# Queueing the rotary multiply-adds behind the next projection piece, not right after the half copies that feed them

## The chip, the cores and the metric

The kernel runs on the eight cores of one Trainium2 chip; each core computes one sequence of the batch with the same program, and no core talks to another. The metric is the device time of the slowest core, in microseconds (us). Most executions agree within 0.3%, but some fall into a slower state in which one die has a lower granted clock. Engines are called PE (matrix multiply), DVE (vector), ACT (scalar activation), POOL (GpSimd) and SP (sync). The granted clock is the share of PE's full clock that its throttle let through, as the trace records it. The program gives each engine its own queue of instructions, in the order in which it emits them.

## The reference

A decoder layer: normalisation, one combined input projection, two kinds of attention side by side, an output projection, and an MLP. This study touches the part below: eight heads of attention over all earlier positions with a forget bias ("fox"), and eight query heads plus two key heads that are rotated ("rope") for sliding-window attention.

```python
def rope(x, pos):                 # rotate-half over 128 dimensions, half = 64
    ...
    x1, x2 = xf[..., :half], xf[..., half:]
    out = jnp.concatenate([x1 * cos - x2 * sin, x2 * cos + x1 * sin], axis=-1)

def reference(...):
    h = rmsnorm(x, g_pre_mix) * (1.0 + sc_a) + sh_a
    proj = h @ w_in                                  # 2048 x 2048 by 2048 x 4616, per sequence
    fq, fk, fv, fg, sq, sk, sv = split(proj)
    fox = forgetting_attention(fq, fk, fv, log_f)    # 8 heads, causal
    sq = rope(sq); sk = rope(sk)                     # 8 + 2 heads: ten "stripes" of 128 columns
    swa = sliding_window_sink_attention(sq, sk, sv, sinks)
    x = x + gt_a * rmsnorm(concat(fox, swa) @ w_out, g_post_mix)
    ...                                              # squared-ReLU MLP
```

## The kernel before

The program interleaves two streams. The attention of fox heads 0 and 1 is the steady stream; each of its steps has a score matmul (PE), a subtraction of the forget bias (DVE), an exponential (ACT) and two matmuls that use it (PE). Between these, a filler emits pieces of the projections: one piece is four matmuls, and a 512-column tile of a stripe takes four pieces.

```python
    def fox(segs):                           # LA = 3 steps of lookahead
        ...
            if i + LA < n:
                begin(i + LA)                # score matmul into a bank of SF = [2, 3, 5]
            F.fill(w)                        # w = 5.6 matmuls: 1 or 2 pieces
            pv(L[i])                         # two matmuls that use exp of step i
            if i + LA < n:
                expo(L[i + LA])              # DVE subtraction, then ACT exp
            F.fill(w)

    def g_fm(slot, t, evac, rel):            # one tile of a projection stripe, in 4 pieces
        bk = next_pj()                       # projection banks 0 and 1 in turn
        for q in range(4):
            pe([... 4 matmuls into bk ...])
            if q == 3:
                ...
                evac(bk)
            yield 4
```

The rotary evacuation of a tile is the function that was changed. ACT copies the two halves crosswise into `rot`; then DVE makes two multiply-adds (each adds the bias and multiplies by the cosine or the sine) and an addition of them.

```python
    def ev_rope(i, dstf):
        def mk(t):
            ...
            def ev(bk):
                rot, cs = rots[rp[0] % 2], sqb[rp[0] % 2]
                rp[0] += 1
                act(rot(p=(0, 64)), bk(p=(64, 128)), AF.Copy)
                act(rot(p=(64, 128)), bk(p=(0, 64)), AF.Copy)
                stt(cs(), bk(), bs(slice(i, i + 1)), cosT(sl), ALU.add, ALU.mult)
                stt(rot(), rot(), bsw(slice(i, i + 1)), sinT(sl), ALU.add, ALU.mult)
                tt(dstf(sl), cs(), rot(), ALU.add)
            return ev
        return mk
```

At a stripe's start, its bias column is computed by 16 one-column matmuls into the bank that the next score matmul will use, and copied out by DVE (the "bias copy", `bs`). That score matmul must wait for this copy.

```python
    def sw_bias(i, b):
        bk = fm_col(b, banks[SF[St.sb % 3]])          # calls col(): 16 small matmuls
        cp(bs(slice(i, i + 1)), bk(0, 1))             # DVE: the bias copy
        act(bsw(...), bs(...), AF.Copy)               # ACT, twice: the halves crosswise
        ...
```

The order on DVE follows from this: score subtractions, rotary ops and bias copies stand in one queue, and an instruction whose input is late holds up all that follow. What counts as late is set by the program: its `op()` makes a reader of a PSUM bank (where matmul results land) wait for the last reader of that bank on another engine. So the first rotary op waits for both half copies, although it uses nothing that they write.

The softmax here doesn't subtract the row's maximum and nothing guards it: scores larger than these inputs give would overflow.

Of the kernel before, what the change touches and what calls it, by code (L numbers as in the profile page):

```python
# [9 lines left out]
ALU = mybir.AluOpType  # L10
# [328 lines left out]
def program(nc, stack, orders, dry, T):  # L339
# [20 lines left out]
    shb, bq, bqb, bs, bsw, bvb, bsv, wob = (B[n] for n in ("shb", "bq", "bqb", "bs", "bsw", "bvb", "bsv", "wob"))  # L360
# [3 lines left out]
    cosT, sinT = B["cosT"], B["sinT"]  # L364
# [15 lines left out]
    def mm(out, lhsT, rhs, start, stop):  # L380
        return (out.ap, lhsT.ap, rhs.ap, start, stop)

    def pe(mms, r, w, extra=()):
        def fn(e):
            ins = None
            for (o, l, rh, st, sp) in mms:
                ins = e.matmul(o, lhsT=l, rhs=rh, start=st, stop=sp)  # L387
            return ins
        return P.op("pe", fn, r, w, extra=extra)

    def act(out, in_, func, bias=None, scale=1.0):
        r = [in_]
        kw = {}
        if isinstance(bias, Acc):
            r.append(bias)
            kw["bias"] = bias.ap
        elif bias is not None:
            kw["bias"] = bias
        if isinstance(scale, Acc):
            r.append(scale)  # L400
            kw["scale"] = scale.ap
        else:
            kw["scale"] = scale
        return P.op("act", lambda e: e.activation(out=out.ap, in_=in_.ap, func=func, **kw), r, [out])  # L404

    def tt(out, a, b, op, eng="dve"):
        return P.op(eng, lambda e: e.tensor_tensor(out=out.ap, in0=a.ap, in1=b.ap, op=op), [a, b], [out])  # L407

    def stt(out, a, s, b, op0, op1, eng="dve"):
        r = [a, b] + ([s] if isinstance(s, Acc) else [])  # L410
        sc = s.ap if isinstance(s, Acc) else s
        return P.op(eng, lambda e: e.scalar_tensor_tensor(out=out.ap, in0=a.ap, scalar=sc, in1=b.ap, op0=op0, op1=op1),  # L412
                    r, [out])
# [6 lines left out]
    def cp(out, a):  # L420
        return P.op("dve", lambda e: e.tensor_copy(out=out.ap, in_=a.ap), [a], [out])  # L421
# [121 lines left out]
    def next_pj():  # L543
        b = banks[PJ[pj[0] % 2]]
        pj[0] += 1
        return b
# [13 lines left out]
    def g_v(slots, bp, dst, rel, add=None):  # L560
        bk = next_pj()
        for bi in range(2):
            blk = 2 * bp + bi
            t, o = blk // 4, (blk % 4) * 128
            for q in range(2):
                b = R1.bufs[slots[q]]
                pe([mm(bk(bi * 256, bi * 256 + 256), hT(t, 8 * q + kk, slice(o, o + 128)), b(slice(kk * 256, kk * 256 + 256)),
                       q == 0 and kk == 0, q == 1 and kk == 7) for kk in range(8)],
                   [b()] + [hT(t, slice(8 * q, 8 * q + 8))], [bk()])
                if bi == 1 and rel:  # L570
                    R1.rel(slots[q])
                if bi == 1 and q == 1:
                    src = bk()
                    src = src.re(src.ap.rearrange("p (a d) -> p a d", a=2))
                    if add is None:
                        cp(dst(slice(2 * bp, 2 * bp + 2)), src)
                    else:
                        tt(dst(slice(2 * bp, 2 * bp + 2)), src, add().re(add.h[:].unsqueeze(1).broadcast_to([128, 2, 256])), ALU.add)
                yield 4


    def col(out, slot_bufs, lhs):

        bk = out or next_pj()
        pe([mm(bk(0, 1), lhs(k), shb(slice(k, k + 1)), k == 0, k == KC - 1) for k in range(KC)], slot_bufs + [shb()], [bk()])
        return bk

    def fm_col(b, out=None):
        return col(out, [b()], lambda k: b(slice(k * 128, k * 128 + 128)))
# [27 lines left out]
    def ev_rope(i, dstf):  # L617
        def mk(t):
            sl = slice(t * TS, t * TS + TS)

            def ev(bk):
                rot, cs = rots[rp[0] % 2], sqb[rp[0] % 2]
                rp[0] += 1
                act(rot(p=(0, 64)), bk(p=(64, 128)), AF.Copy)
                act(rot(p=(64, 128)), bk(p=(0, 64)), AF.Copy)
                stt(cs(), bk(), bs(slice(i, i + 1)), cosT(sl), ALU.add, ALU.mult)
                stt(rot(), rot(), bsw(slice(i, i + 1)), sinT(sl), ALU.add, ALU.mult)
                tt(dstf(sl), cs(), rot(), ALU.add)
            return ev
        return mk  # L630

# [7 lines left out]
    def v_col(p, s):  # L639
        for hh in range(2):  # L640
            bk = col(None, [R1.bufs[x]() for x in s],
                     lambda k: R1.bufs[s[k // 8]](slice((k % 8) * 256 + hh * 128, (k % 8) * 256 + hh * 128 + 128)))
            cp(bvb(slice(2 * p + hh, 2 * p + hh + 1)), bk(0, 1))
# [13 lines left out]
        yield 2  # L657

    def svpair():
        s = [R1.acq(("A", I_SV)), R1.acq(("A", I_SV + 1))]  # L660
        bk = next_pj()
        pe([mm(bk(0, 256), shb(slice(k, k + 1)).re(shb.h[:, k:k + 1].broadcast_to([128, 128])),
               R1.bufs[s[k // 8]](slice((k % 8) * 256, (k % 8) * 256 + 256)), k == 0, k == KC - 1) for k in range(KC)],
           [R1.bufs[x]() for x in s] + [shb()], [bk()])
        cp(bsv(), bk(0, 256))
        for bp in range(8):
            yield from g_v(s, bp, vts, bp == 7, bsv)
# [10 lines left out]
    class Fill:  # L678
        def __init__(self):
            self.main = []  # L680
            self.side = []
            self.every = 4
            self.n = 0
            self.pend = []
            self.credit = 0.0

        def _one(self):
            while self.main:
                try:
                    v = next(self.main[0])  # L690
                except StopIteration:
                    self.main.pop(0)
                    continue
                self.n += 1
                if self.n % self.every == 0:
                    self._side()
                return v
            return None
# [20 lines left out]
        def drain(self):  # L719
            while self.main:  # L720
                self._one()
            self.credit = 0.0

        def drain_side(self):
# [3 lines left out]
    F = Fill()  # L728
# [384 lines left out]
    def qk_(h):  # L1113
# [3 lines left out]
        for t in range(NT):  # L1117
# [4 lines left out]
    F.every = 6  # L1122
    F.side = [mods(g, F.pend) for g in range(2, 6)]
    fox([(0, lambda: [sk_(0), svpair(), sq_(0), sq_(1), sq_(2), sq_(3)], 64 * 5 + 128, 0),
         (1, lambda: [sk_(1), sq_(4), sq_(5), sq_(6), sq_(7), qk_(2)], 64 * 7, 0)])
    F.drain()
# [241 lines left out]
def build():  # L1368
# [117 lines left out]
    with ExitStack() as stack:  # L1486
        T["banks"] = [Bank(stack.enter_context(nc.psum_tensor(f"bank{i}", [128, 512], F32)), i) for i in range(8)]
        orders = program(nc, stack, {}, True, T)
        program(nc, stack, orders, False, T)
# [49 lines left out]
```

## Time and profile before

| | before |
|---|---|
| time, median of 3 executions | 3128.81 us (3125.04 to 3580.78, the last slow) |
| the stretch: first bias copy to first sliding-window matmul, mean of 8 cores | 320.1 us |
| PE idle in it (core 3) | 34.9 us |
| DVE waiting for half copies in it (core 3) | 105.9 us |

From the page of the kernel before: busy time and its share of the span, then the span in 40 slices (tenths busy; granted PE clock in tenths), then the engines' shares of the chain that ended last.

```profile
PE 2913.8 (93%) x15016; PEld 1375.2 (44%) x15016; DVE 928.1 (30%) x1489; ACT 748.4 (24%) x1224; POOL 469.1 (15%) x614
...
PE   2799989999999899999999999999999999999993
...
PEclk9899989999999899999999999999999999999996
...
PE 82%; DVE 5%; DMA 4%; ACT 4%; issue 3%; POOL 1%; SPq 0%; DVEq 0%; ACTq 0%; POOLq 0%
```

PE has work for 93% of the time. The stretch with the rotary stripes is slices 3 to 7, counted from 0 (a slice is 78 us); in the middle of it, in slice 5, both the PE row and the clock row show an 8.

The windows view of core 3 over the stretch. Columns: busy time and instructions of each engine, granted clock, DMA share, GB/s.

```profile
core 3: us, PE busy (x) PEld busy (x) DVE busy (x) ACT busy (x) POOL busy (x), PEclk, DMA share, GB/s
273.50:595.90 322.40, 287.49 (x1625) 137.41 (x1624) 146.29 (x240) 110.34 (x197) 25.36 (x48) 0.91 0.49 85
```

PE is busy 287.5 of 322.4 us at a mean clock of 0.91; DVE is busy 45% and ACT 34%.

The waits view of the same stretch, PE first (who waited for whom, us in total, times, longest), then DVE.

```profile
PE bank L387 <- DVE bs L421: 23.0, 8, 5.0
PE bank L387 <- DVE sq_207 L412: 6.2, 2, 3.2
PE bank L387 <- DVE modT L407: 3.8, 2, 3.4
```

```profile
DVE sq_206 L412 <- ACT qrot L404: 63.7, 20, 8.0
DVE sq_207 L412 <- ACT acc_208 L404: 42.2, 20, 2.7
```

Two thirds of PE's idle time ends with a copy of 128 single values. DVE waits 105.9 us for half copies, 40 times. (`sq` is the tile that the first rotary op writes, `qrot` and `acc` are the two buffers for `rot`; `modT` holds modulation vectors that the filler computes as a side job.)

The chain of waits of the kernel before shows one rotary tile, from one exponential to the next (start us, length us, what; some tiny hand-overs left out).

```profile
371.69 0.45 ACT Pb_101 L404
...
372.40 0.59 ACT acc_208 L404
...
373.01 0.60 ACT acc_208 L404
...
373.70 0.75 DVE sq_207 L412
374.45 0.67 DVE acc_208 L412
...
375.22 0.10 DVE mix L407
...
375.83 0.70 DVE bank L407
...
376.61 0.55 ACT Pb_102 L404
```

ACT makes an exponential (Pb), then the two half copies (acc is one of the two buffers for `rot`); only then DVE can make its three rotary ops, and only after these the score subtraction (bank) that the next exponential needs. One turn takes 4.92 us (371.69 to 376.61), and each engine is idle for most of the other's part.

The PE timeline at the first stripe boundary (in brackets, the idle time before an instruction and what ended it).

```profile
356.43 0.54 PE L387 MATMUL bank<-shb,ring_69 128*128 128x1 bf16 x16
356.83 1.02 PE L387 MATMUL bank<-hT,ring_69 128*128 128x512 bf16 x4
361.37 0.58 PE L387 MATMUL bank<-qT_72,kT_73 128*128 128x512 bf16 x1 [3.51 <-DVE bs L421]
361.75 1.91 PE L387 MATMUL bank<-hT,ring_69 128*128 128x512 bf16 x4
```

The bias column ends at 356.8 us, a projection piece follows, then PE stands still for 3.51 us until the bias copy is done, and afterwards four matmuls take 1.91 us instead of 1.02.

### The profile page before, as it was taken

What the parts mean: (1) busy time and instruction counts of PE and PEld (TensorE: products, weight loads), DVE (VectorE), ACT (ScalarE), POOL (GpSimd) and SP (SyncE); (2) the same over time, 40 slices, a digit from 0 to 9 for tenths busy, and PEclk for the clock granted to TensorE, in tenths of its full rate; (3) what the DMA queues carried; (4) which work ended last, traced back from release to release, by engine and by line L of the source; (5) the groups of instructions that cost most, each with busy time, mean ns of one, the idle gap of its engine ahead of it and who ended that gap; (6) DMA issues with size and microseconds to landing.
All of it is one profiled execution on the core that took longest, in us unless ns stands there. A gap on an engine that the chain in (4) does not pass through costs nothing.

```text
span 3124.7 us, 38905 instructions; the slowest of 8 cores (3109.0 to 3124.7 us)
## 1 busy us (share of the span) xinstructions
PE 2913.8 (93%) x15016; PEld 1375.2 (44%) x15016; DVE 928.1 (30%) x1489; ACT 748.4 (24%) x1224; POOL 469.1 (15%) x614
## 2 busy tenths in 40 slices
PE   2799989999999899999999999999999999999993
PEld 1336533466444344444444444444444444444441
DVE  1323445345555456642111000000233211000005
ACT  1312333454555435532111000000111111000000
POOL 1010000000001155520000011111100000111114
PEclk9899989999999899999999999999999999999996
DMA  9855545433646324354444455555788544444455
GB/s 185 215 90 104 101 75 88 78 61 59 112 85 102 77 95 157 127 130 74 78 78 74 82 100 95 96 92 96 162 189 191 92 75 78 77 75 77 78 99 197
DMA packets 99782, 327.92 MB, mean 105 GB/s; under 512 B 12144, under 2 KB 12272, under 8 KB 93200
## 3 DMA queue, kind: packets, MB, share of 16 engines
q0 software_dynamic: 58896, 213.97, 41.6%
q1 hardware_dynamic: 40704, 111.46, 10.2%
q8 instruction: 122, 2.00, 0.3%
q14 instruction: 60, 0.49, 0.1%
HBM read 497.32 MB, written 42.01 MB: 173 GB/s over the span
## 4 chain that ended last, share of the span: by engine, by line
PE 82%; DVE 5%; DMA 4%; ACT 4%; issue 3%; POOL 1%; SPq 0%; DVEq 0%; ACTq 0%; POOLq 0%
PE bank L387 82%; DVE bank L407 1%; POOL acc_209 L407 1%; DMA xstA<-xP 1%; DMA xstB<-xP 1%; DMA rmod_87<-wMA 1%; ACT acc_208 L404 1%; DVE mixF L412 1%; ACT rr L404 1%; DMA cfb_82<-crow 1%; ACT qrot L404 1%; DMA rsh_90<-wMB 0%; DVE bank L412 0%; DVE sq_207 L412 0%; DVE acc_208 L412 0%
## 5 line engine op out<-in xcount | busy, mean ns | idle before, releaser
L418 DVE TENSOR_SCALAR bank<-bank 128x512 f32<-128x512 f32 x256 | 166.1, 695 | 638.4 <-PE bank L387 638.4
L421 DVE COPY mixF<-bank 128x512 f32<-128x512 f32 x64 | 41.3, 686 | 842.8 <-PE bank L387 842.8
L387 PE MATMUL bank<-mix,rung_130 128*128 128x512 bf16 x1024 | 226.2, 379 | 0.0
L387 PE MATMUL bank<-mix,rung_127 128*128 128x512 bf16 x1024 | 226.2, 379 | 0.0
L387 PE MATMUL bank<-mix,rung_128 128*128 128x512 bf16 x1024 | 226.2, 379 | 0.0
L387 PE MATMUL bank<-mix,rung_129 128*128 128x512 bf16 x1024 | 226.2, 379 | 0.0
L404 ACT ACTIVATE sq_206<-bank 128x512 f32<-128x512 f32 x30 | 17.9, 598 | 792.9 <-DVE mixF L421 792.9
L387 PEld LDWEIGHTS bank<-mix,rung_129 128*128 128x128 bf16 x1024 | 100.2, 98 | 121.5 <-issue 1.1
L387 PEld LDWEIGHTS bank<-mix,rung_127 128*128 128x128 bf16 x1024 | 100.3, 98 | 120.7
L387 PEld LDWEIGHTS bank<-mix,rung_128 128*128 128x128 bf16 x1024 | 100.4, 98 | 120.7
L387 PEld LDWEIGHTS bank<-mix,rung_130 128*128 128x128 bf16 x1024 | 99.9, 98 | 121.5 <-issue 0.6
L407 DVE TENSOR_TENSOR bank<-bank,cfb_82 128x512 f32<-128x512 f32 x192 | 117.3, 629 | 85.2 <-PE bank L387 80.6
L387 PE MATMUL bank<-hT,ring_69 128*128 128x512 bf16 x512 | 139.6, 404 | 3.2 <-DVE sq_207 L412 3.2
L387 PE MATMUL bank<-hT,ring_71 128*128 128x512 bf16 x384 | 101.7, 394 | 0.4 <-DVE kT_73 L421 0.4
L407 POOL TENSOR_TENSOR acc_208<-acc_208,sq_206 128x512 f32<-128x512 f32 x62 | 78.6, 1267 | 113.1 <-ACT sq_206 L404 113.0
L407 DVE TENSOR_TENSOR bank<-bank,cfb_80 128x512 f32<-128x512 f32 (+3 forms) x128 | 73.5, 594 | 39.2 <-PE bank L387 39.2
L407 POOL TENSOR_TENSOR acc_209<-acc_209,sq_207 128x512 f32<-128x512 f32 x62 | 78.3, 1262 | 45.0 <-ACT sq_207 L404 43.1
L387 PE MATMUL bank<-qT_93,kT_94 128*128 128x512 bf16 (+3 forms) x160 | 57.4, 359 | 24.3 <-DVE bs L421 14.2
L387 PEld LDWEIGHTS bank<-hT,ring_69 128*128 128x128 bf16 x512 | 51.0, 103 | 61.3 <-issue 16.9
L387 PE MATMUL bank<-qT_72,kT_73 128*128 128x512 bf16 (+3 forms) x160 | 57.1, 359 | 18.9 <-DVE bs L421 8.8
L387 PE MATMUL bank<-hT,ring_68 128*128 128x512 bf16 x256 | 67.1, 394 | 1.1 <-DVE kT_73 L421 1.1
L387 PE MATMUL bank<-hT,ring_67 128*128 128x512 bf16 x192 | 58.9, 393 | 0.0
(759 smaller groups left out, 4803.5 us busy)
## 6 DMA issues: line engine op xcount, KB each, us to landing
rung_127<-wU POOLq DMA_DIRECT2D x32, 512.0 KB, 5.3
rung_128<-wU POOLq DMA_DIRECT2D x32, 512.0 KB, 5.3
rung_129<-wU POOLq DMA_DIRECT2D x32, 512.0 KB, 5.2
rung_130<-wU POOLq DMA_DIRECT2D x32, 512.0 KB, 5.4
rung_127<-wD POOLq DMA_DIRECT2D x32, 512.0 KB, 5.2
rung_128<-wD POOLq DMA_DIRECT2D x32, 512.0 KB, 5.3
rung_129<-wD POOLq DMA_DIRECT2D x32, 512.0 KB, 5.3
rung_130<-wD POOLq DMA_DIRECT2D x32, 512.0 KB, 5.7
```

The source lines that it names most:

```text
L387: ins = e.matmul(o, lhsT=l, rhs=rh, start=st, stop=sp)
L404: return P.op("act", lambda e: e.activation(out=out.ap, in_=in_.ap, func=func, **kw), r, [out])
L407: return P.op(eng, lambda e: e.tensor_tensor(out=out.ap, in0=a.ap, in1=b.ap, op=op), [a, b], [out])
L412: return P.op(eng, lambda e: e.scalar_tensor_tensor(out=out.ap, in0=a.ap, scalar=sc, in1=b.ap, op0=op0, op1=op1), r, [out])
L418: return P.op(eng, lambda e: e.tensor_scalar(out=out.ap, in0=a.ap, scalar1=sc, scalar2=None, op0=op), r, [out])
L421: return P.op("dve", lambda e: e.tensor_copy(out=out.ap, in_=a.ap), [a], [out])
```

## The change

The intent: let DVE do something useful while ACT copies. The three rotary ops are put on a list and emitted when the filler's count of pieces (`F.n`) has gone up by two, which is after the next piece and ahead of the one after it, so that a score subtraction can be emitted ahead of them. The list is emptied early where a new column or the token-major projection (that of the sliding-window values) begins.

```diff
     def col(out, slot_bufs, lhs):
 
+        F._late(1 << 30)
+        F._late(1 << 30)
         bk = out or next_pj()
 ...
-                stt(cs(), bk(), bs(slice(i, i + 1)), cosT(sl), ALU.add, ALU.mult)
-                stt(rot(), rot(), bsw(slice(i, i + 1)), sinT(sl), ALU.add, ALU.mult)
-                tt(dstf(sl), cs(), rot(), ALU.add)
+
+                def rest():
+                    stt(cs(), bk(), bs(slice(i, i + 1)), cosT(sl), ALU.add, ALU.mult)
+                    stt(rot(), rot(), bsw(slice(i, i + 1)), sinT(sl), ALU.add, ALU.mult)
+                    tt(dstf(sl), cs(), rot(), ALU.add)
+                F.late.append((F.n + 2, rest))
 ...                                    # svpair(): the same two flush lines
+        def _late(self, n):
+            while self.late and self.late[0][0] <= n:
+                self.late.pop(0)[1]()
+
         def _one(self):
+            self._late(self.n)
             while self.main:
 ...                                    # drain() empties the list too
```

More of the change, by code (lines that the diff above doesn't have):

```diff
@@ L659, in svpair @@
     def svpair():
+        F._late(1 << 30)
+        F._late(1 << 30)
         s = [R1.acq(("A", I_SV)), R1.acq(("A", I_SV + 1))]
@@ L684, in __init__ @@
             self.pend = []
+            self.late = []
             self.credit = 0.0
+        def _late(self, n):
+            while self.late and self.late[0][0] <= n:
+                self.late.pop(0)[1]()
         def _one(self):
+            self._late(self.n)
             while self.main:
@@ L721, in drain @@
                 self._one()
+            self._late(1 << 30)
             self.credit = 0.0
```

## The prediction

> **What bounds the kernel now.** TensorE: 93% busy, 82% of the chain of waits. The change touches only the rotary stretch, 278 to 557 us. There (windows view, 275 to 560) PE is busy 250 of 285 us, DVE 138, ACT 101, granted clock 0.91; later dense stretches have 1.00. Lost there:
> - Idle PE, about 36 us. By the waits view 23.0 us (8 waits) end with the tiny bias copy (DVE bs) at a stripe's start, 6.2 us (2) with a rotary op freeing a projection bank, 3.4 us with modT.
> - After most of these stalls four 512-column matmuls take 1.9 instead of 1.03 us (timeline), for 3 to 4 us. The Trainium skill, "TensorE: Matmul & The Clock Gate", section "What's actually happening", names a half-rate clock after idling; this trace agrees (0.66 in slices after the longest stalls).
> - The undisturbed stripe (338.1 to 356.4 us) takes 18.3 us, about 4.7 per tile with a margin; the others average some 24.
>
> So 50 to 55 us (1.7%) is the ceiling.
>
> **What the change does.** It adds and removes no operation. 40 times, three rotary ops on DVE (0.75 + 0.74 + 0.69, about 2.1 us in sequence) move behind one more projection piece (four matmuls, 0.87 us), so that a score subtraction (0.69) may pass them. Today the chain of waits (366 to 387 us) shows ACT and DVE taking turns: exp 0.6, two half copies 1.2, rotary 2.1, subtraction 0.7: 4.9 us per tile, 5.5 with two subtractions, against PE's 4.7. DVE waits 106 us for the half copies (40 waits). By my count of pieces a subtraction lands between copies and rotary ops for 5 of 7 tiles, which brings the turn-taking to about 4.4 us per tile, an estimate, below PE's need.
>
> **How much is critical.** Less than those 106 us suggest. The turn-taking builds a backlog of only 0.2 to 0.8 us a tile. Most of the loss is at a stripe's start, where the next score matmul needs the bias column's bank, freed by the bias copy, which queues behind the last tile's copies and rotary ops: 1.2 + 2.1 + 0.15, with handovers 3.7 us. The change flushes its queue before that column, so this order stays. The first such boundary (361 us) follows a stripe without backlog, and still costs 3.5 us; I reckon 2.8 after. So I expect some nine boundary stalls to shrink by 0.7 to 1.5 us each, not to vanish: 7 to 13 us of idle. Some then become too short to bring the half clock: 4 to 8 us more. The waits before the token-major projection (298 us) and after the last rotary stripe (557 us) stay. Later stages only start earlier.
>
> **Prediction:** 3112 us, 17 less than 3128.8; 3092 to 3130 should hold it 8 times in 10. Faster by over 2%: 0.02; within 2%: 0.965; slower by over 2%: 0.015.
>
> **What would show each step.**
> - DVE's waits for the half copies fall from 106 to some 50 us.
> - PE's waits on bs stay about 8 and fall from 23 to 10-16 us.
> - The clock of 338-557 us rises from 0.90 to about 0.94; the stretch 278-557 shortens by 12 to 22 us; what follows keeps its length within 5 us.
>
> **What would make it wrong.** If backlog rather than the boundary order makes the stalls, waits on bs vanish and up to 55 us are won (3075). If boundary stalls and half clock stay, nothing changes. Deferred rotary ops hold a projection bank longer (of two), and PE might wait for it; I expect not, since the bank is next needed three pieces later.

## More of the kernel before

"The stretch" is used as a ruler all through this document. Its ends are read from the tile view: the start of the first `bs` copy, and of the first matmul on `mix` and `skT`, on each core of the profiled execution.

## The result, and the profile after

| | before | after |
|---|---|---|
| time, median | 3128.76 us (4 executions) | 3098.45 us (3097.49 to 3100.45, 4 executions) |
| the stretch, mean of 8 cores | 320.1 us | 291.6 us |
| what follows the stretch, mean of 8 cores | 2524.6 us | 2526.2 us |
| PE idle in the stretch (core 3) | 34.9 us | 18.6 us |
| DVE waiting for half copies (core 3) | 105.9 us | 59.3 us |

The ratio of the two is 0.9908, with a 95% interval from 0.9888 to 0.9927. Ratios here are formed from fast executions of the same rounds, so not quite the ratio of the medians quoted (the median before has a slow execution among its four). The whole gain of some 30 us lies in the stretch, which is 28.5 us shorter; the rest kept its length.

The page of the changed kernel (its slowest core is core 5), same lines as before:

```profile
PE 2898.8 (94%) x15016; PEld 1371.8 (44%) x15016; DVE 929.4 (30%) x1489; ACT 750.9 (24%) x1224; POOL 469.1 (15%) x614
...
PE   2799999999998899999999999999999999999993
...
PEclk9899999999999999999999999999999999999997
...
PE 84%; DVE 5%; DMA 4%; ACT 3%; issue 3%; POOL 1%; SPq 0%; DVEq 0%; POOLq 0%; ACTq 0%
```

The 8 of slice 5 is a 9 now in both rows, and PE has a larger part of the chain (84 instead of 82%). For the stretch, core 3 again, so that the same core is compared; the windows view:

```profile
273.90:564.90 291.00, 272.38 (x1625) 133.81 (x1623) 147.64 (x240) 111.48 (x197) 25.35 (x48) 0.97 0.56 95
```

The same 1625 matmul instructions took 272.4 us busy instead of 287.5, at a clock of 0.97 instead of 0.91. So of the 31.4 us that this core won, 16.3 are idle time and 15.1 are a faster pace of PE. The waits view, PE and DVE:

```profile
PE bank L387 <- DVE bs L421: 15.4, 7, 2.8
PE bank L387 <- DVE sq L412: 2.3, 2, 1.5
PE bank L387 <- DVE modT L407: 0.9, 2, 0.4
```

```profile
DVE sq L412 <- ACT acc L404: 30.1, 17, 2.4
...
DVE sq L412 <- ACT qrot L404: 29.2, 20, 2.7
```

PE's waits on the bias copy fell by a third, from 23.0 to 15.4 us, and the other two nearly went. The timelines of DVE and of ACT (core 3) show what the new order does in a tile.

```profile
369.70 0.69 DVE L407 TENSOR_TENSOR bank<-bank,cfb 128x512 f32<-128x512 f32 x1
371.47 0.70 DVE L407 TENSOR_TENSOR bank<-bank,cfb 128x512 f32<-128x512 f32 x1 [1.08 <-PE bank L387]
372.54 0.75 DVE L412 SCALAR_TENSOR_TENSOR sq<-bank,bs,cosT 128x512 f32<-128x512 f32 x1 [0.37 <-ACT qrot L404]
```

```profile
371.25 1.19 ACT L404 ACTIVATE qrot<-bank 64x512 f32<-64x512 f32 x2
372.47 0.69 ACT L404 ACTIVATE Pb<-bank,Ctok 128x512 bf16<-128x512 f32 x1
375.56 1.20 ACT L404 ACTIVATE acc<-bank 64x512 f32<-64x512 f32 x2 [2.41 <-PE bank L387]
```

DVE makes the subtraction at 371.47 us while ACT is busy with the half copies, so the rotary op waited only 0.37 us; and ACT finds the input of its next exponential (372.47 us) ready right after the copies. Before the next copies (375.56) ACT is idle for 2.41 us, and what ends that is PE, no more DVE. The boundary of the first stripe:

```profile
352.44 0.54 PE L387 MATMUL bank<-shb,ring 128*128 128x1 bf16 x16
...
356.67 0.38 PE L387 MATMUL bank<-qT,kT 128*128 128x512 bf16 x1 [2.81 <-DVE bs L421]
```

It was 3.51 us and is 2.81.

Comparing the order of the instructions on DVE before and after shows that in 26 of the 40 tiles one subtraction has passed ahead of the rotary ops.

### The profile page after: what moved, and what is told of

It is laid out like the page before. It is cut to its first block, busy times and chain, and to the rows that moved or that the text cites. A ratio compares the mean times of both kernels' runs of the same rounds, so it can differ in the third digit from the quotient of the medians.

```text
span 3098.5 us, 38921 instructions; the slowest of 8 cores (3086.4 to 3098.5 us)
## 1 busy us (share of the span) xinstructions
PE 2898.8 (94%) x15016; PEld 1371.8 (44%) x15016; DVE 929.4 (30%) x1489; ACT 750.9 (24%) x1224; POOL 469.1 (15%) x614
## 4 chain that ended last, share of the span: by engine, by line
PE 84%; DVE 5%; DMA 4%; ACT 3%; issue 3%; POOL 1%; SPq 0%; DVEq 0%; POOLq 0%; ACTq 0%
PE bank L387 84%; POOL acc L407 1%; DVE bank L407 1%; DMA xstA<-xP 1%; DMA xstB<-xP 1%; DMA rmod<-wMA 1%; ACT Pb L404 1%; DVE mixF L412 1%; DVE bank L412 1%; ACT rr L404 1%; DMA rsh<-wMB 0%; ACT sq L404 0%; ACT acc L404 0%; DVE sq L412 0%; DVE Y L407 0%
## 5 line engine op out<-in xcount | busy, mean ns | idle before, releaser
L387 PE MATMUL bank<-mix,rung 128*128 128x512 bf16 x4096 | 884.9, 379 | 0.0
L387 PE MATMUL bank<-a,rung 128*128 128x512 bf16 x4096 | 884.4, 379 | 0.0
L387 PEld LDWEIGHTS bank<-mix,rung 128*128 128x128 bf16 x4096 | 400.8, 98 | 484.3 <-issue 1.7
L387 PEld LDWEIGHTS bank<-a,rung 128*128 128x128 bf16 x4096 | 400.8, 98 | 483.3
L387 PE MATMUL bank<-hT,ring 128*128 128x512 bf16 x1536 | 404.0, 388 | 3.0 <-DVE sq L412 1.5
L404 ACT ACTIVATE Pb<-bank,Ctok 128x512 bf16<-128x512 f32 (+1 forms) x320 | 194.3, 626 | 292.1 <-DVE bank L407 289.6
L407 POOL TENSOR_TENSOR acc<-acc,sq 128x512 f32<-128x512 f32 x180 | 225.3, 1266 | 220.7 <-ACT sq L404 216.1
L387 PE MATMUL bank<-mix,WO 128*128 128x512 bf16 x1024 | 235.8, 384 | 13.8 <-ACT sq L404 12.5
L407 DVE TENSOR_TENSOR bank<-bank,cfb 128x512 f32<-128x512 f32 (+1 forms) x320 | 191.5, 616 | 140.4 <-PE bank L387 136.0
L387 PE MATMUL bank<-ring,hT 128*128 128x256 bf16 x1280 | 172.6, 279 | 5.5 <-DVE bvb L421 2.4
```

The costliest lines, as they stand in the source:

```text
L387: ins = e.matmul(o, lhsT=l, rhs=rh, start=st, stop=sp)
L404: return P.op("act", lambda e: e.activation(out=out.ap, in_=in_.ap, func=func, **kw), r, [out])
L407: return P.op(eng, lambda e: e.tensor_tensor(out=out.ap, in0=a.ap, in1=b.ap, op=op), [a, b], [out])
```

## The experiments

Two theories stood against each other. The *boundary theory*, which the prediction leaned on, has PE lose its time at stripe starts, where the bias copy stands behind the last tile's copies and rotary ops. The *turn-taking theory* (called backlog theory in the first expectations) has the turns of ACT and DVE set the pace of the whole stretch; PE's waits only show up at the stripe starts. All kernels of the experiments passed the reference, except e9, which is wrong.

| run | edit | stretch, mean of 8 cores | time of fast executions | ratio to before, 95% |
|---|---|---|---|---|
| before | | 320.1 | 3125.0 to 3128.8 | |
| changed | | 291.6 | 3097.5 to 3100.5 | 0.9908 [0.9888, 0.9927] |
| e3_midonly | changed, last tile of a stripe not deferred | 291.4 | 3095.7 to 3099.6 | 0.9906 [0.9887, 0.9925] |
| e2_lastonly | only last tile deferred, past the bias copy | 297.9 | 3104.4 to 3106.3 | 0.9932 [0.9909, 0.9954] |
| e1_noflush | changed, bias column does not flush | 271.2 | 3076.1 to 3080.6 | 0.9846 [0.9826, 0.9865] |
| e6_defer1 | e1 with delay 1 | 309.7 | 3112.8 to 3112.9 | 0.9960 [0.9936, 0.9984] |
| e7_defer4 | e1 with delay 4 | 277.6 | 3083.8 to 3084.5 | 0.9868 [0.9845, 0.9892] |
| e8_noflushpool | e1, addition on POOL | 266.7 | 3070.1 to 3072.9 | 0.9829 [0.9805, 0.9852] |
| e5_beforepool | before, addition on POOL | 288.5 | 3093.1 to 3094.9 | 0.9900 [0.9876, 0.9924] |
| e9_onecopy | before, one copy instead of two (wrong result) | 290.2 | 3095.5 to 3099.7 | 0.9902 [0.9884, 0.9919] |
| e12_between | before, useless copy between the two | 351.3 | 3154.5 to 3158.5 | see text |
| e10_threecopies | before, useless copy after the two | 322.9 | 3129.2 and 3140.3 | 1.0022 [0.9990, 1.0053] |
| e11_changedthree | changed, useless copy after the two | 294.0 | 3098.5 to 3098.6 | none formed |
| e4_beforewarm | before, useless matmuls at stripe starts | 316.3 | 3124.5 to 3126.6 | 0.9996 [0.9974, 1.0019] |

### Taking the change apart: e1, e2, e3

e1_noflush (the bias column of a rotary stripe passes a bank of its own as `out`, so it no longer flushes):

```diff
     def col(out, slot_bufs, lhs):
 
-        F._late(1 << 30)
-        F._late(1 << 30)
+        if out is None:
+            F._late(1 << 30)
```

> The changed kernel, but the bias column at a stripe's start no longer empties the queue of deferred rotary ops, so the bias copy on DVE goes ahead of the last tile's rotary ops. Boundary theory (what is left is lost at stripe starts, because the bias copy queues behind the last tile's half copies and rotary ops): PE's waits on bs fall from 15.4 us to under 5, the half clock after them disappears, and the time falls by another 15 to 22 us, to about 3080. Backlog theory (PE loses time because copies and rotary ops take turns all through the stripe, and stripe starts are only where it shows): the change has already cured that, waits on bs fall little, time within 5 us of 3098.

The boundary theory's number came out, 3079.18 us median, and the backlog theory's (within 5 us of 3098) did not. The waits view of its slowest core (7), PE:

```profile
PE bank L387 <- DVE sq L412: 3.6, 4, 1.5
...
PE bank L387 <- DVE bs L421: 0.8, 1, 0.8
```

The waits on the bias copy are gone, and single-us windows show no half clock after the first few us of the stretch. So the flush ahead of the bias column, which the changed kernel still has, costs another 20.4 us of stretch: by the order on DVE the bias copy now stands ahead of the last tile's rotary ops at 8 of the ten stripe starts, and a subtraction passes in 29 tiles instead of 26. But this does not say that boundaries were what the change itself had cured.

e2_lastonly, on top of e1:

```diff
-                F.late.append((F.n + 2, rest))
+                if t == NT - 1:
+                    F.late.append((F.n + 2, rest))
+                else:
+                    rest()
```

> As e1_noflush, but only the last tile of each stripe is deferred; the other three keep the order of the kernel before. Boundary theory: most of the gain is here: waits on bs below 8 us, time 3085 to 3100. Backlog theory: three of four tiles still take turns with ACT, so under a third of the changed kernel's 30 us is won: 3118 to 3128.

The fast executions, 3104.4 to 3106.3 us, lie between the two expectations. The PE waits (core 1, its slowest):

```profile
PE bank L387 <- DVE sq L412: 12.0, 10, 4.4
...
PE bank L387 <- ACT Pb L404: 4.2, 3, 2.8
PE bank L387 <- DVE bs L421: 2.0, 2, 1.2
```

The waits on the bias copy went as the boundary theory has it, but the waits on rotary ops that free a bank rose to 12.0 us (6.2 before): PE now caught up with the turn-taking engines elsewhere. Still, the stretch is 22.2 us shorter than before, although a subtraction passes in only 7 of the 40 tiles. So letting the bias copy go ahead at the stripe starts is a cure of its own, worth over two thirds of what the change won, and the backlog theory, which allowed it less than a third, falls in its strict form too. The two cures do not exclude each other; which one the change applies is for e3 to say.

e3_midonly, on the changed kernel:

```diff
-                F.late.append((F.n + 2, rest))
+                if t < NT - 1:
+                    F.late.append((F.n + 2, rest))
+                else:
+                    F._late(1 << 30)
+                    rest()
```

> The changed kernel, but the last tile of each stripe is not deferred; the other three are. Boundary theory in its strict form (backlog adds nothing): waits on bs stay near 23 us, time 3120 to 3128. Backlog theory: nearly the whole gain stays, 3098 to 3105. My mixed expectation: the deferral of the last tile ends after one piece anyway and its order against the bias copy is unchanged, so nearly all of the changed kernel's gain is backlog taken away: 3100 to 3106, waits on bs 15 to 18 us.

291.4 us against 291.6 (and 3095.7 to 3099.6 us, at or just below the lower end of what the theories that keep the gain expected): the deferral of the last tile adds nothing, and the waits on the bias copy stay at 15.9 us. The gain of the change is that of the tiles inside the stripes. As an account of this change, the strict boundary theory falls.

### Changing the length of the turn, not the order: e5, e9, e10, e12

e5_beforepool, on the kernel before: `tt(dstf(sl), cs(), rot(), ALU.add, eng="pool")`.

> The kernel before, in its old order, with the third rotary op (the addition, 0.69 us on DVE, 40 of them) on GpSimd instead. No subtraction passes anything; the turn between ACT and DVE just gets 0.7 us shorter, 4.9 to about 4.2 us per tile, and so does the queue ahead of the bias copy. Turn-taking theory (the length of this turn sets the pace of the stripes): the stretch from the first bias copy to the first sliding-window matmul (mean of eight cores 320.1 us before, 291.6 changed, 271.2 in e1_noflush) falls to 285 to 300, time 3098 to 3110. If it is only the order that matters (a subtraction must be able to pass), it stays above 312, time over 3118.

The windows view of core 3:

```profile
272.00:561.00 289.00, 271.11 (x1625) 133.31 (x1624) 120.28 (x200) 110.47 (x197) 75.75 (x88) 0.97 0.57 95
```

The stretch fell to 288.5 us in the mean of the cores (the time, 3093.1 to 3094.9, to a little below the expected 3098 to 3110). Nothing passed anything; the turn was merely shorter by one DVE instruction of 0.69 us, and 40 times that are 27.6 us, against 31.6 won.

e9_onecopy, on the kernel before:

```diff
-                act(rot(p=(0, 64)), bk(p=(64, 128)), AF.Copy)
-                act(rot(p=(64, 128)), bk(p=(0, 64)), AF.Copy)
+                act(rot(), bk(), AF.Copy)
```

> The kernel before with one 128-partition copy in place of the two half copies (the halves are not swapped, so the result is wrong on purpose); order unchanged. The turn gets about 0.6 us shorter on ACT instead of on DVE. Turn-taking theory: the engine on which the turn is shortened is all the same, so as in e5_beforepool (288.5 us) the stretch falls to 285 to 296 us. If it were the load of DVE that counted in e5_beforepool, the stretch stays above 312.

```profile
274.50:565.60 291.10, 273.94 (x1624) 134.00 (x1622) 146.33 (x240) 85.06 (x157) 25.35 (x48) 0.96 0.56 93
```

290.2 us in the mean of the cores (above, core 3: DVE is busy 146.33 us, before 146.29, and ACT 85.06 instead of 110.34): shortening the turn on the other engine, with DVE's work unchanged, is worth nearly the same. It is not the load of DVE.

e10_threecopies adds `act(rot(p=(0, 64)), rot(p=(0, 64)), AF.Copy)` after the two half copies.

> The kernel before with a third, useless half copy on ACT (in place, about 0.6 us with its wait). Turn-taking theory: 36 to 40 tiles pay 0.6 to 0.7 us each, the stretch grows from 320 to 340 to 352 us, time 3148 to 3160. If only stripe starts counted, ten of them pay: 326 to 330 us.

This expectation failed: 322.9 us, hardly more than before. The timelines of ACT and of DVE (core 0) show why.

```profile
370.27 1.19 ACT L404 ACTIVATE qrot<-bank 64x512 f32<-64x512 f32 x2
371.56 0.63 ACT L404 ACTIVATE qrot<-qrot 64x512 f32<-64x512 f32 x1
```

```profile
371.56 0.75 DVE L412 SCALAR_TENSOR_TENSOR sq<-bank,bs,cosT 128x512 f32<-128x512 f32 x1 [2.09 <-ACT qrot L404]
372.29 0.75 DVE L412 SCALAR_TENSOR_TENSOR qrot<-qrot,bsw,sinT 128x512 f32<-128x512 f32 x1
```

The useless copy and the first rotary op start at the same time, 371.56 us: that op reads the bank, which by the rule of `op()` only the two real copies keep from it, and the second rotary op, which does need `rot`, starts 0.73 us later, when the useless copy (0.63) has ended. So 0.63 us of ACT work per tile that lies beside the turn is nearly free (2.8 us of stretch in all). The second of the two fast executions, 3140.33 us, had two cores at a lower clock (0.965 and 0.968), so I go by the stretch.

e12_between puts the same line between the two half copies, where it delays the last reader of the bank.

> e10_threecopies again, with the useless in-place copy put between the two half copies. There it could hide beside the first rotary op, which reads the bank and not the copied halves (it ended before the second one needed it); here the last half copy, which is the last reader of the bank that the first rotary op waits for, comes 0.65 to 0.75 us later. Turn-taking theory: the turn grows from 4.92 to about 5.6 us per tile, the stretch from 320 to 340 to 352 us. If the pace were not set by this turn, it stays within 5 us of 323 as in e10_threecopies.

DVE's timeline (core 1) and the windows view (core 3):

```profile
375.70 0.75 DVE L412 SCALAR_TENSOR_TENSOR sq<-bank,bs,cosT 128x512 f32<-128x512 f32 x1 [2.82 <-ACT qrot L404]
...
381.34 0.75 DVE L412 SCALAR_TENSOR_TENSOR sq<-bank,bs,cosT 128x512 f32<-128x512 f32 x1 [2.83 <-ACT acc L404]
```

```profile
274.20:626.90 352.70, 291.50 (x1625) 138.20 (x1624) 146.30 (x240) 135.85 (x237) 25.35 (x48) 0.89 0.45 78
```

The wait of the first rotary op for the copies is 2.82 us, 0.73 more than in the kernel before (2.09 at 368.78 us of its timeline), and the stretch has grown by 31.2 us, to 351.3; 40 times 0.73 are 29. PE's clock fell to 0.89. The time is 3156.15 us median, against 3126.64 and 3127.27 for the two undisturbed executions of the kernel before on that chip, 0.9% more. The computed ratio (1.0045, interval 0.9934 to 1.0157) takes in a third execution of the kernel before, 3155.98 us, that counts as fast although its die 0 ran at a clock of 0.962 to 0.969; I go by the other two and by the stretch.

So the same line of code, of the same length, costs 2.8 us in one place and 31.2 in the other. Three ways of making the turn 0.6 to 0.7 us shorter or longer moved the stretch by 30 to 32 us each. That is the turn-taking theory's number. The turn ahead of the bias copy was changed as well in each of them, but ten stripe starts at 0.7 us would be 7 us, an estimate, and not 30.

e11_changedthree, the line of e10 on the changed kernel:

> The changed kernel with the same third half copy. Where a subtraction has passed (26 of 40 tiles by the order on DVE) the copies run beside it, and PE's need of 4.7 us per tile leaves some slack: the stretch grows by less than half of what e10_threecopies costs, by 6 to 13 us from 291.6 (the ten stripe starts, whose order is unchanged, pay 0.65 each). If the deferral did nothing for the turns, it grows as much as in e10_threecopies, by 20 or more.

294.0 us, 2.4 more, below the expected 6 to 13. As e10 showed, this copy lies outside the turn, so the run says nothing on the slack of the changed kernel. No ratio was formed; two of its four executions were slow.

### How far to defer: e6, e7

Both are e1_noflush with `F.n + 1` and `F.n + 4` in place of `F.n + 2`.

> e1_noflush with a delay of one piece instead of two. By the count of pieces a subtraction then lands between copies and rotary ops for 5 of 14 tiles instead of 10. Turn-taking theory: turns are broken half as often; the stretch lies between e2_lastonly and e1_noflush, 275 to 290 us, time 3084 to 3098. If the plain delay matters and not the subtraction that passes, one piece does as well as two: within 3 us of 271.

309.7 us, outside what either theory expected, because I had overlooked something: with a delay of one the list is emptied at the beginning of the next piece, ahead of the bias column, so the bias copy stands behind the last tile again. The waits (core 2):

```profile
PE bank L387 <- DVE bs L421: 23.0, 8, 4.8
```

They are those of the kernel before. Its proper comparison is e3_midonly, which has the same order at the boundaries. By the order on DVE a subtraction passes in 12 tiles in e6 and in 22 in e3; the stretch is 309.7 and 291.4 us, against 320.1 with none. This fits the number of passes: too short a delay lets too little pass.

> e1_noflush with a delay of four pieces: a subtraction passes for every tile, and the projection bank is held up to the piece before its next use. Turn-taking theory: little is left to win (PE idle in the stretch is 6.3 us in e1_noflush), 264 to 272 us, time 3072 to 3080. If holding the bank costs something: PE waits for the rotary op that frees it (3.6 us in e1_noflush) rise over 8 us and the stretch gets longer than 274.

277.6 us, 6.4 longer than with a delay of two, although now a subtraction passes in all 40 tiles. What the last sentence of the expectation names has happened (core 4, PE's waits):

```profile
PE bank L387 <- DVE sq L412: 11.3, 7, 2.2
```

PE waits 11.3 us, against 3.6 in e1, for rotary ops that free a projection bank. Longer is not better.

### The half clock by itself: e4

e4_beforewarm puts 16 useless 256-column matmuls into unread columns of the bias bank after each bias column of the kernel before.

> The kernel before with 16 useless 256-column matmuls (1.7 us) into unread columns of the bias bank after each bias column: they fill part of the wait for the bias copy with PE work and change no order on DVE or ACT. If half of the changed kernel's 30 us came from the half clock after stalls (half-clock time 51 us before, 14 us after in this stretch, so about 18 us of work time), then keeping PE busy wins 10 to 18 us with DVE waiting as long for half copies as before (3111 to 3119). If the half clock follows something else than idling, nothing is won, or up to 15 us are lost to the added matmuls (3129 to 3144).

The windows view of its stretch on core 3:

```profile
279.20:595.10 315.90, 288.25 (x1769) 147.94 (x1768) 146.21 (x240) 110.36 (x197) 25.35 (x48) 0.97 0.51 86
```

The mean clock rose from 0.91 to 0.97, as much as in the changed kernel, and the time hardly moved (ratio 0.9996): that is what the second expectation had, but not for its reason, since the clock did follow the idling. The stretch is 3.8 us shorter in the mean of the cores, 6.5 on this one; but the first 16 useless matmuls lie ahead of the ruler, where they ran at half clock for 3.6 us, and so hide about as much. The other 144 are the difference between 1769 and 1625. PE was busy 288.25 us; less those 144 (0.109 us each from start to start, 15.7 together) that is 272.6 for the work that took 287.5 before. So 14.9 us of pace were won, but the idle time is 27.7 us: with 15.7 of the old 34.9 filled, 19.2 should have been left, so 8.4 us of waiting came back. DVE still waited 99.8 us for half copies. This suggests that a good part of the lost pace was not on the critical path as long as ACT and DVE set it. How much exactly cannot be said from this run, since the useless matmuls also delay real pieces.

### The version that beats both: e8

e8_noflushpool joins e1 and e5.

> e1_noflush with the rotary addition on GpSimd. If turns still cost anything, up to 4 us are won (3075); if PE now sets the pace, nothing: within 3 us of 3079.

It is the fastest, 3070.07 to 3072.86 us in its three fast executions. Its stretch is 266.0 to 267.6 us on the eight cores, e1's 270.4 to 271.9; the two ran at different times, and their intervals against the kernel before overlap. In the mean its fast executions are 7.5 us below e1's, more than either expectation allowed; its stretch is 4.5 us shorter. PE idles 2.7 us in the stretch on core 3, so little is left there. One side effect shows in the tile view (min/median/max ns on core 2):

```profile
L407 DVE TENSOR_TENSOR mix<-acc,rr x32: 691/693/1172, 288.8 to 1033.3; 128x512 bf16<-128x512 f32 x32
```

This DVE addition, 693 ns otherwise, takes up to 1172. The Trainium skill, "SBUF — State Buffer", section "SBUF: two separate sides", says that a DVE instruction with two SBUF inputs and a GpSimd instruction that reads SBUF use a shared port pair, which one holds while the other blocks. This trace agrees: of the eight such DVE additions in the stretch on core 2, the three that started during one of POOL's additions (1.26 us each) took 0.76, 0.80 and 1.17 us, and the other five 0.69; in the kernel before none of the 32 took over 0.693. No run was made to isolate it.

## Why the prediction was right or wrong

The direction, the range (3092 to 3130) and the class (within 2%) were right, the expected size was not: 17 us, and 30 measured. That 3098 fell into the range is in part luck: the range was wide, and its lower part was reached by the turn-taking, which the text had made small. Point by point:

- **Right: where.** The stretch took all of the gain, and what follows it moved by 1.6 us. The ceiling of 50 to 55 us held: e8 won 53 us of stretch. The stretch itself was to shorten by 12 to 22 us, and did by 28.5.
- **Right: the first boundary.** "I reckon 2.8 after": 2.81 us. Waits on the bias copy: expected about 8 waits and 10 to 16 us, measured 7 and 15.4. The flush does keep that order, and e1 shows that it costs 20 us.
- **Nearly right: what passes.** "5 of 7 tiles", 26 of 40 by the order on DVE. DVE's waits for half copies fell to 59 us, "some 50" expected.
- **Wrong: "How much is critical. Less than those 106 us suggest. The turn-taking builds a backlog of only 0.2 to 0.8 us a tile. Most of the loss is at a stripe's start".** I compared the turn (4.9 us) with PE's need (4.7) as if PE were the pacemaker and the turn a small excess. But 0.2 to 0.8 us a tile, times 40 tiles, is already 8 to 32 us (an estimate from the prediction's own figures, which it did not make); e3, in which the order at the boundaries is the old one, won 28.7 us, 0.72 a tile. The turn was the pacemaker, and PE's stops at stripe starts were in large part PE waiting for it. e5, e9 and e12 show it: 0.6 to 0.7 us per tile, either way, on either engine, are worth 30 us of stretch. The boundary did have some 20 us of its own to give (e1, e2), but the change leaves its order alone, as the prediction itself said. The term "7 to 13 us of idle" measured 16.3. Of that, 7.6 are the waits on the bias copy, in line with the text; most of the rest are other waits: those on rotary ops before the token-major projection and after the last stripe, which it said would stay, fell from 6.2 to 2.3 us, and those on modT from 3.8 to 0.9.
- **Wrong: the size of the clock term.** "4 to 8 us more", measured 15.1. I took 3 to 4 us of half pace per stall. By the clock records of core 3 in the kernel before, five stalls of 3.2 to 5.0 us were followed by 6.8 us at a lower clock, five of 2.3 to 3.0 us by 3.4 us. Shortening the first boundary's stall from 3.5 to 2.8 us so halved what follows it. Lower clock in the stretch fell from 56.3 to 18.4 us. But e4 warns against counting this as a separate gain: with that clock nearly restored and the turns untouched, the stretch got only 3.8 us shorter, although the useless matmuls blur this.

The idle and busy terms are how the won time shows on PE; the cause, as far as these runs show, is that the turn got shorter. That the gain of the change is that of the passing subtractions rests on e3 and e6 (0, 12 and 22 passes: 320.1, 309.7, 291.4 us) together with e5, e9 and e12. What stays open is the exact worth of one pass: it is not the same for all (12 passes won 10.4 us, 22 won 28.7), perhaps because PE's own need caps some; no run shows that.

## What to carry to other kernels

Two engines that are each less than half busy can set the pace together, when each one's next instruction waits for the other's last; look in the chain of waits for the cycle, measure its length, and ask what can be taken out of it or passed ahead. An instruction's place relative to that cycle decides its price: the same 0.6 us copy cost 2.8 us beside it and 31 us inside it. When you defer work, look also at what still waits behind it (here a tiny copy behind a flush, worth another 20 us), and stop before the held buffer is needed again.

## What the Trainium skill lacked or had wrong

- "TensorE: Matmul & The Clock Gate", section "What's actually happening", gives a half-rate state and a window of about 3.4 us. The runs agree: on core 3 before and after, all lower-clock stretches after the first stripe had begun were 3.4 or 6.8 us long, and the clock in them 0.50. Its section "Why this matters for your kernels" advises no idle gaps over about 3 us; here gaps of 2.11 and 2.46 us in the changed kernel were each followed by 3.4 us of half clock (core 3, 466 and 442 us), while another of 2.46 us (423 us) was not. Shorter gaps than that advice allows can do it. What told them apart was their place: on this core the clock changed only at multiples of 3.41 us from one another, and the gaps at 442 and 466 us lie inside one such step, while the one at 423 is cut in two, 1.23 us in each; that fits the first section's word for the window, free-running. On this core steps with 2.11 us or more of idle time were followed by half clock, and steps with 1.90 or less were not.
- "Perfetto Trace Analysis", section "Identifying the Most-Contended Engine", would look for the engine with the highest occupancy and optimise that first. In this stretch DVE was 45% and ACT 34% busy, PE 89%, and the gain lay in the turn of the two less busy ones (0.7 us per tile for 30 us). (The section wants PE's headroom judged by MFU and by the busy share of its weight loads, the latter here 137.41 of 322.4 us or 43%; that puts PE beside DVE and still does not point to a turn.) The same page's "Optimization Strategy", to go from the gaps of the busy engine to what blocks it, does lead there, but the page says nothing of a cycle between two engines whose waits are then charged to a third instruction.
- No page that I read says that restoring the granted clock may win little while something else sets the pace: in e4 it rose from 0.91 to 0.97, the stretch got 3.8 us shorter, and the time hardly moved (ratio 0.9996).
